# Identity built on GpSimd, the norm's weights loaded as one row and spread by two matmuls of ones

## The chip, the cores and the metric

The kernel runs on one core of one Trainium2 chip. The time is the device time of one execution in microseconds (us); the change is judged by the median of several executions. TensorE is called PE in the profile, VectorE DVE, ScalarE ACT, GpSimd POOL, and SP is the engine that issues most DMAs.

## What is computed

One decoder block on 1024 tokens of width 1024: a SwiGLU half-step, a merge of dilated attention and pooling, a second half-step, and a final norm. Only the first lines matter here, since the change lies in the norm ahead of the first half-step:

```
def rms_norm(x, g):
    xf = x.astype(jnp.float32)
    y = xf * lax.rsqrt(jnp.mean(xf * xf, axis=-1, keepdims=True) + RMS_EPS)
    return (y * g.astype(jnp.float32)).astype(x.dtype)

h = h + 0.5 * swiglu(rms_norm(h, ffn1_norm[l]), ffn1_w1[l], ffn1_w3[l], ffn1_w2[l])
```

`ffn1_norm` holds one weight per channel, 1024 in all. Everything behind this norm is left as it is.

## The kernel before

Tokens are tiled by 128: `h[0]` to `h[7]` hold the rows of `x`, one token per partition, 1024 channels along the partition. The matrix products are done in fp32 split in a high and a low part, by a scheme that multiplies halves (tokens 0 to 511 and 512 to 1023; channels 0 to 511, `LOWS`, and 512 to 1023, `HIGHS`). The first products need the transpose of the LOWS half of the first four row tiles; it is called `b11`.

The order of every engine's instructions in this stage is written out by hand in `begin_up1`. For each row tile t of the first four:

1. `squares(t)`: ACT squares the row and sums it (L274), once the row's DMA has landed.
2. `inverse(t)`: DVE forms mean plus epsilon (L278), POOL raises it to the power -0.5 (L279). The result is the tile `nst`.
3. `rows(t, "b11", LOWS)`: DVE multiplies the half row by `nst` and by the norm's weights (L285, a SCALAR_TENSOR_TENSOR). PE transposes the four 128x128 blocks by a product with the identity `ident` (L407) into a PSUM bank `x_b`. ACT copies the bank into the high part `xhi_b` (L408), and later DVE subtracts to get the low part `xlo_b` (L411, `lower`).

When all four are transposed, `entry.product` starts the first real products (`u_f10a`, L331). Between these steps stand calls of `keep_on(n)`: n products of ones with ones into a bank named `idle` (L916) that nobody reads. Each shows as two MATMUL rows in the profile. PE takes its instructions in order, so what stands behind them waits for them.

The weights have to lie along the free dimension on all 128 partitions for step 3. They come as a 128x8 tile `gain1` (one DMA on ACT's queue, 32 bytes per partition). DVE widens each column to 128 equal columns (`widen`, L920), PE transposes the eight blocks (`gains`, L926), which leaves the weights spread over all partitions in two PSUM banks, one for LOWS and one for HIGHS. DVE copies the first bank into the SBUF tile `gain_row` (L942), ACT later the second (L960). The identity is loaded by a second DMA on ACT's queue (L871).

SP issues the loads of rows and of the first weights, in program order. A DMA takes one of eight semaphores in turn, and is issued when the DMA eight places ahead of it has landed.

SBUF has a left and a right stack of pools. `consts` is the lowest pool on the left. It holds `ident`, `ones`, `mhalf`, `gain1` and two unused tiles named `pad`; the operands `xhi`, `xlo` and the left operands of the down products lie above it.

Of the kernel before, what the change touches and what calls it, by code (L numbers as in the profile page):

```python
# [10 lines left out]
F32 = mybir.dt.float32  # L11
F32R = mybir.dt.float32r
AF = mybir.ActivationFunctionType
OP = mybir.AluOpType
AX = mybir.AxisListType

P = 128
# [3 lines left out]
KT = D // P  # L21
# [116 lines left out]
def tile_block(  # L138
# [28 lines left out]
    nc = tc.nc  # L167
    ve, ac, gp, pe = nc.vector, nc.scalar, nc.gpsimd, nc.tensor

    def sbuf(name, side="left", bufs=1):  # L170
        return tc.tile_pool(name=name, bufs=bufs, side=side, reuse_waits="tile")

    consts = ctx.enter_context(sbuf("consts"))
# [5 lines left out]
    def bank(tag, name):  # L179
        return psum.tile([P, HALF], F32, tag=tag, name=name)  # L180

    def tmp(name):
        return keep.tile([P, 1024], F32, tag="tmp", bufs=TMP_BUFS, name=name)
# [9 lines left out]
    ident = consts.tile([P, P], F32, name="ident")  # L193
    ones = consts.tile([P, P], F32, name="ones")
# [4 lines left out]
    h = []  # L199
# [70 lines left out]
    inv = {}  # L270

    def squares(t, out):
        inv[t] = small.tile([P, 2], F32, tag="nst", name=f"nst_{t}")
        ac.activation(out, h[t], AF.Square, accum_out=inv[t][:, 0:1])  # L274

    def inverse(t):
        st = inv[t]
        ve.tensor_scalar(st[:, 0:1], st[:, 0:1], 1.0 / D, EPS, op0=OP.mult, op1=OP.add)  # L278
        gp.tensor_tensor(st[:, 1:2], st[:, 0:1], mhalf, op=OP.pow)  # L279

    def scaled(t, out, gain):
        ve.scalar_tensor_tensor(out, h[t], inv.pop(t)[:, 1:2], gain, op0=OP.mult, op1=OP.mult)

    def scaled_part(t, c, gain):
        ve.scalar_tensor_tensor(h[t][:, c], h[t][:, c], inv[t][:, 1:2], gain[:, c], op0=OP.mult, op1=OP.mult)  # L285
# [12 lines left out]
    LOWS, HIGHS = slice(0, HALF), slice(HALF, S)  # L298
# [564 lines left out]
                    tick(i)  # L863


    gain1 = consts.tile([P, KT], F32, name="gain1")
    warm = consts.tile([P, 1], F32, name="warm")
    cnt = consts.tile([P, 4, 16], F32, name="cnt")
    psc = consts.tile([P, 4], F32, name="psc")
    nc.scalar.dma_start(gain1, ffn1_norm)  # L870
    nc.scalar.dma_start(ident, c_ident)  # L871
    ac.activation(warm, mhalf, AF.Silu)

    scope = ExitStack()
# [9 lines left out]
    gain_row = keep.tile([P, D], F32, tag="gain", bufs=1, name="gain_ffn1")  # L884
    square = row("square")
    columns_tile = tmp("columns")
    columns = columns_tile.rearrange("p (k c) -> p k c", k=KT)

    def load_all():
        load_rows(0, 1, 2, 3)  # L890
        raws.depth = 2
        raws.load()
        load_rows(4)
        raws.depth = 3
        raws.load()
        load_rows(5)
        raws.depth = 4
        raws.load()
        load_rows(6, 7)
        raws.depth = 6  # L900
        raws.load()

    def pre_run(sv, todo, first, low):
        return Entry(sv, [(*((q.A, m, q.a_out), (q.B, m, q.b_out))[k],) for q, m in todo for k in range(2)], low,
                     lambda n, part=0: first.A.summed(6, part > 1, gp) if part else first.A.operand((6, 7)[n]))

    def begin_up1():


        load_all()  # L910
        idle = bank("mm", "idle")

        def keep_on(n):

            for _ in range(n):
                pe.matmul(idle[:, :P], ones, ones, start=True, stop=True)  # L916

        def widen(b):
            k = slice(4 * b, 4 * b + 4)
            ve.tensor_copy(columns[:, k], gain1[:, k, None].to_broadcast([P, 4, P]))  # L920

        def gains(b):

            p = bank("acc", f"gain{b}")
            for k in range(4):
                pe.transpose(p[:, k * P:(k + 1) * P], columns[:, 4 * b + k], ident)  # L926
            return p

        r = {}

        def rows(t, what, c, tag="acc"):
            scaled_part(t, c, gain_row)
            r[t] = Rows(X, what, h[t][:, c], t, tag)

        keep_on(12)
        widen(0)
        squares(0, square)
        widen(1)
        inverse(0)
        g = [gains(b) for b in range(2)]  # L940
        keep_on(2)
        ve.tensor_copy(gain_row[:, LOWS], g[0])  # L942
        for t in range(1, 4):
            squares(t, square)
        inverse(1)
        rows(0, "b11", LOWS)
        keep_on(2)
        rows(1, "b11", LOWS)
        inverse(2)
        inverse(3)  # L950
        keep_on(2)
        pairs = [Pair(sv1, j, sums, True, j == 2) for j in range(3)]
        entry = pre_run(sv1, [(q, m) for m in (1, 2) for q in pairs[:2]] + [(pairs[2], m) for m in (1, 2)],
                        pairs[0], h[:4])
        entry.operand(0)
        rows(2, "b11", LOWS)
        keep_on(3)
        rows(3, "b11", LOWS, "mm")
        keep_on(2)
        ac.activation(gain_row[:, HIGHS], g[1], AF.Copy)  # L960
        for t in range(4):
            r[t].lower()
        sv1.terms = (0, 2, 1)
        entry.product(0)
        sv1.terms = (0, 1, 2)
        entry.operand(1)
        for t in range(4):
            r[t].keep(h[t][:, LOWS])

        square2 = columns_tile  # L970
        squares(4, square2)
        for t in (0, 1):
            rows(t, "b21", HIGHS)
        entry.product(1)
        entry.out(0)
        entry.operand(2)
        entry.operand(3)
        inverse(4)
        r[0].lower()
        for t in (2, 3):  # L980
            rows(t, "b21", HIGHS)
        for t in (1, 2):
            r[t].lower()
        entry.product(2)
        entry.out(1)
        squares(5, square2)
        r[3].lower()
        for t in range(4):
            r[t].keep(h[t][:, HIGHS])
        entry.product(3)  # L990
        entry.operand(4)
        entry.out(2)
        entry.operand(5)
        entry.out(3)

        def high(t, part):
            if part == 0:
                inverse(t)
                return
            scaled(t, h[t], gain_row)  # L1000
            return h[t]

        def after(t):
            if t + 2 < NT:
                squares(t + 2, square2)
            if t < 6:
                raws.depth = t + 3
                raws.load()

        entry.run(high, after, 4)  # L1010
        return pairs
# [406 lines left out]
    with tc.manual_schedule():  # L1418
# [4 lines left out]
        for k in range(len(items) + 4):  # L1423
# [7 lines left out]
            if k < len(items):  # L1431
                q, m = items[k]
# [3 lines left out]
            if k - 1 in results:  # L1436
                q, m = items[k - 1]
# [358 lines left out]
    def branches():  # L1796
        for n in range(2 * KT):
            yield from branch(n)

    fill = branches()  # L1800
# [65 lines left out]
    first = first_w_o()  # L1866
# [193 lines left out]
    with tc.manual_schedule():  # L2060
# [28 lines left out]
        for i in range(2, STEPS - 4):  # L2089
            step_o(i)  # L2090
            m, st = i // 2 - 1, i % 2
# [13 lines left out]
        m = len(DOWN) - 1  # L2105
# [18 lines left out]
        r = [rows_first2(t) for t in range(2)]  # L2124
# [223 lines left out]
```

## Time and profile before

| | |
|---|---|
| median of 3 runs | 1892.95 us (1892.79 to 1893.48) |
| time of the profiled execution | 1892.07 us |
| its span | 1890.2 us |
| PE busy | 1879.9 us, 99% of the span |
| granted PE clock, mean | 0.999 |
| bytes moved by DMA | 330.79 MB, mean 175 GB/s |

The span is the time from the first to the last record on the core. A row of the timeline has the start in us, the busy time in us, the engine, the line, the operation with out and in, the count of instructions merged into the row, and in brackets the idle time ahead of it with what ended it. A merged row's time runs from its first start to its last end.

### The profile page before, as it was taken

What the parts mean: (1) busy time and instruction counts of PE and PEld (TensorE: products, weight loads), DVE (VectorE), ACT (ScalarE), POOL (GpSimd) and SP (SyncE); (2) the same over time, 40 slices, a digit from 0 to 9 for tenths busy, and PEclk for the clock granted to TensorE, in tenths of its full rate; (3) what the DMA queues carried; (4) which work ended last, traced back from release to release, by engine and by line L of the source; (5) the groups of instructions that cost most, each with busy time, mean ns of one, the idle gap of its engine ahead of it and who ended that gap; (6) DMA issues with size and microseconds to landing.
All of it is one profiled execution on the core that took longest, in us unless ns stands there. A gap on an engine that the chain in (4) does not pass through costs nothing.

```text
span 1890.2 us, 24694 instructions
## 1 busy us (share of the span) xinstructions
PE 1879.9 (99%) x8822; PEld 1561.9 (83%) x8822; DVE 1331.9 (70%) x1975; ACT 772.8 (41%) x1394; POOL 712.2 (38%) x533
## 2 busy tenths in 40 slices
PE   9999999999999999999999999999999999999998
PEld 8888888888888888888888888888888888888887
DVE  6776556657786777557885896887665566577867
ACT  7323333333334553334445772363333323334344
POOL 5433333331223254444555357543333333312221
PEclk9999999999999999999999999999999999999999
DMA  5154223436566526765668968744332223454654
GB/s 191 60 198 166 84 89 106 139 111 216 170 224 210 183 84 210 236 219 188 224 236 314 322 224 289 270 153 149 140 127 103 84 102 118 137 189 162 226 197 145
DMA packets 144019, 330.79 MB, mean 175 GB/s; under 512 B 17560, under 2 KB 39064, under 8 KB 142360
## 3 DMA queue, kind: packets, MB, share of 16 engines
q1 hardware_dynamic: 140152, 318.36, 48.6%
q10 hardware_dynamic: 3744, 10.85, 1.6%
q8 instruction: 70, 1.15, 0.3%
q14 instruction: 53, 0.43, 0.1%
HBM read 229.61 MB, written 99.55 MB: 174 GB/s over the span
## 4 chain that ended last, share of the span: by engine, by line
PE 57%; DVE 2%; ACT 1%; DMA 1%; issue 0%; POOL 0%; ACTq 0%; DVEq 0%; SPq 0%
PE u_mixm L331 15%; PE d_f L815 11%; PE wo L2028 4%; PE yp L1770 1%; PE u_f20b L331 1%; PE u_f21a L331 1%; PE u_f210b L331 1%; PE u_f210a L331 1%; PE u_f29b L331 1%; PE u_f29a L331 1%; PE u_f28a L331 1%; PE u_f27b L331 1%; PE u_f27a L331 1%; PE u_f26b L331 1%; PE u_f26a L331 1%; PE u_f25b L331 1%
## 5 line engine op out<-in xcount | busy, mean ns | idle before, releaser
L815 PE MATMUL d_f<-bhi_f,ahi_f 128*128 128x512 f32 x616 | 240.2, 390 | 0.0
L815 PE MATMUL d_f<-bhi_f,alo_f 128*128 128x512 f32 x616 | 239.7, 389 | 0.0
L815 PE MATMUL d_f<-blo_f,ahi_f 128*128 128x512 f32 x616 | 239.6, 389 | 0.0
L772 POOL TENSOR_TENSOR alo_f<-g_f,ahi_f 128x512 fp32r<-128x512 f32 x60 | 85.9, 1448 | 270.0 <-ACT ahi_f L768 270.0
L331 PE MATMUL u_mixm<-xhi_t_mix,wc_mixm 128*128 128x512 f32 x608 | 157.3, 391 | 0.1
L815 PEld LDWEIGHTS d_f<-bhi_f,ahi_f 128*128 128x128 f32 x616 | 115.7, 188 | 24.2 <-ACT h L415 0.5
L815 PEld LDWEIGHTS d_f<-bhi_f,alo_f 128*128 128x128 f32 x616 | 115.6, 188 | 24.2
L815 PEld LDWEIGHTS d_f<-blo_f,ahi_f 128*128 128x128 f32 x616 | 115.7, 188 | 23.7
L331 PEld LDWEIGHTS u_mixm<-xhi_t_mix,wc_mixm 128*128 128x128 f32 x608 | 113.5, 188 | 23.9 <-ACT wc_mixm L319 0.7
L331 PE MATMUL u_mixm<-xhi_b_mix,wc_mixm 128*128 128x512 f32 x456 | 120.4, 391 | 0.0
L322 POOL TENSOR_TENSOR wc_mixm<-s_mixm,wc_mixm 128x512 fp32r<-128x512 f32 x52 | 76.6, 1475 | 104.9 <-ACT wc_mixm L319 94.0
L331 PEld LDWEIGHTS u_mixm<-xhi_b_mix,wc_mixm 128*128 128x128 f32 x456 | 84.9, 188 | 17.3
L319 ACT ACTIVATE wc_mixm<-s_mixm 128x512 fp32r<-128x512 f32 x76 | 47.0, 628 | 109.4 <-DVE s_mixm L373 54.6
L768 ACT ACTIVATE ahi_f<-g_f 128x1024 fp32r<-128x1024 f32 x84 | 81.9, 975 | 3.1 <-DMA g_f<-gs_f 2.0
L331 PE MATMUL u_mixm<-xlo_t_mix,wc_mixm 128*128 128x512 f32 x304 | 81.3, 389 | 0.0
L322 POOL TENSOR_TENSOR wc_mixm<-raw,wc_mixm 128x512 fp32r<-128x512 f32 x40 | 60.2, 1505 | 40.8 <-ACT wc_mixm L319 32.4
L2028 PE MATMUL wo<-w_o,o_hi 128*128 128x512 f32 x224 | 69.3, 390 | 0.0
L768 ACT ACTIVATE bhi_f<-s_f2w 128x512 fp32r<-128x512 f32 x55 | 33.0, 628 | 86.3 <-DVE s_f2w L790 67.6
L768 ACT ACTIVATE bhi_f<-s_f1w 128x512 fp32r<-128x512 f32 x55 | 33.1, 629 | 83.4 <-DVE s_f1w L790 70.2
L331 PEld LDWEIGHTS u_mixm<-xlo_t_mix,wc_mixm 128*128 128x128 f32 x304 | 57.1, 188 | 12.0
L772 DVE TENSOR_TENSOR alo_f<-g_f,ahi_f 128x1024 fp32r<-128x1024 f32 (+1 forms) x48 | 57.6, 1200 | 7.6 <-ACT ahi_f L768 7.5
L331 PE MATMUL u_mixm<-xlo_b_mix,wc_mixm 128*128 128x512 f32 x228 | 61.0, 389 | 0.0
(1332 smaller groups left out, 4751.9 us busy)
## 6 DMA issues: line engine op xcount, KB each, us to landing
g_f<-gs_f SPq DMA_DIRECT2D x70, 512.0 KB
gs_f<-y_f SPq DMA_DIRECT2D x88, 256.0 KB
raw<-in_w2a_dram SPq DMA_DIRECT2D x35, 512.0 KB
raw<-in_w2b_dram SPq DMA_DIRECT2D x35, 512.0 KB
gs_f<-gb_f SPq DMA_DIRECT2D x46, 256.0 KB
raw<-in_w1a_dram SPq DMA_DIRECT2D x22, 512.0 KB
raw<-in_w3a_dram SPq DMA_DIRECT2D x22, 512.0 KB
raw<-in_w1b_dram SPq DMA_DIRECT2D x22, 512.0 KB
```

The lines of the kernel that those rows point to most:

```text
L319: ac.activation(w[:, 0], src, AF.Copy)
L322: eng.tensor_tensor(w[:, 1], src, w[:, 0].bitcast(F32), op=OP.subtract)
L331: pe.matmul(p, a, b, start=(start and n == 0), stop=(n == 11), skip_group_check=not start)
L768: ac.activation(hi[:, c], src, AF.Copy)
L772: eng.tensor_tensor(lo[:, d], src[:, o], hi[:, d].bitcast(F32), op=OP.subtract)
L815: pe.matmul(self.banks[m][t], l, r, start=(first and q == 0), stop=(last and q == 2))
L1770: pe.matmul(p, a, b, start=(j == 0), stop=(j == 11))
L2028: pe.matmul(banks[m][t], l, r, start=(st == 0 and j == 0 and q == 0), stop=(st == 1 and j == 1 and q == 2))
```

## The change

The identity is made on POOL from the tile of ones (AFFINE_SELECT: keep where partition equals column). The 1024 weights are loaded as one row of 4 KB on one partition (`columns`, in the order p*8+k in which they lie in memory). Two products with a row of ones (contraction over that one partition) spread the row over all partitions into the two PSUM banks; the 512 columns of each are read at a step of 8 elements, 32 bytes, which puts them into channel order. The four scalings of the LOWS half read their weights from the PSUM bank; `gain_row` is filled by ACT afterwards, both halves, for later use. The counts of `keep_on` go from 12 to 7 and from 2 to 3, the banks of x_b 2 come from another tag, and the second scaling stands one `inverse` later. `gain1` is gone, so every tile of the left stack that lies above it starts 32 bytes lower; the right stack is where it was.

```diff
-    gain1 = consts.tile([P, KT], F32, name="gain1")
-    nc.scalar.dma_start(gain1, ffn1_norm)
-    nc.scalar.dma_start(ident, c_ident)
+    gp.affine_select(out=ident, in_=ones, compare_op=OP.is_equal, fill=0.0, base=0, pattern=[[-1, P]],
+                     channel_multiplier=1)
...
-    columns = columns_tile.rearrange("p (k c) -> p k c", k=KT)
+    columns = columns_tile[0:1, :]
+    nc.scalar.dma_start(columns, ffn1_norm.rearrange("(o p) k -> o (p k)", o=1))
...
-        def widen(b):
-            k = slice(4 * b, 4 * b + 4)
-            ve.tensor_copy(columns[:, k], gain1[:, k, None].to_broadcast([P, 4, P]))
-
         def gains(b):
             p = bank("acc", f"gain{b}")
-            for k in range(4):
-                pe.transpose(p[:, k * P:(k + 1) * P], columns[:, 4 * b + k], ident)
+            r = columns.rearrange("o (p k) -> o k p", k=KT)[:, 4 * b:4 * b + 4]
+            pe.matmul(p.rearrange("m (k p) -> m k p", k=4), ones[0:1, :], r, start=True, stop=True)
             return p
...
-        def rows(t, what, c, tag="acc"):
-            scaled_part(t, c, gain_row)
+        def rows(t, what, c, tag="acc", first=None):
+            if first is None:
+                scaled_part(t, c, gain_row)
+            else:
+                ve.scalar_tensor_tensor(h[t][:, c], h[t][:, c], inv[t][:, 1:2], first, op0=OP.mult, op1=OP.mult)
             r[t] = Rows(X, what, h[t][:, c], t, tag)
-        keep_on(12)
-        widen(0)
+        keep_on(7)
         squares(0, square)
-        widen(1)
         inverse(0)
         g = [gains(b) for b in range(2)]
-        keep_on(2)
-        ve.tensor_copy(gain_row[:, LOWS], g[0])
+        keep_on(3)
...
-        rows(0, "b11", LOWS)
+        rows(0, "b11", LOWS, "acc", g[0])
         keep_on(2)
-        rows(1, "b11", LOWS)
         inverse(2)
+        rows(1, "b11", LOWS, "acc", g[0])
         inverse(3)
...
-        rows(2, "b11", LOWS)
+        rows(2, "b11", LOWS, "mm", g[0])
         keep_on(3)
-        rows(3, "b11", LOWS, "mm")
+        rows(3, "b11", LOWS, "mm", g[0])
         keep_on(2)
-        ac.activation(gain_row[:, HIGHS], g[1], AF.Copy)
+        for c, p in zip((HIGHS, LOWS), (g[1], g[0])):
+            ac.activation(gain_row[:, c], p, AF.Copy)
```

On DVE, from the first widening to the fourth scaling, the program before has these rows (x_133 to x_136 are row tiles 0 to 3, and nst_225 to nst_247 their scales):

```order
L920 COPY columns<-gain_109 128x512 x2
L278 TENSOR_SCALAR nst_225<-nst_225 128x1
L942 COPY gain_ffn_141<-gain_230 128x512
L278 TENSOR_SCALAR nst_243<-nst_243 128x1
L285 SCALAR_TENSOR_TENSOR x_133<-x_133,nst_225,gain_ffn_141 128x512
L285 SCALAR_TENSOR_TENSOR x_134<-x_134,nst_243,gain_ffn_141 128x512
L278 TENSOR_SCALAR nst_245<-nst_245 128x1
L278 TENSOR_SCALAR nst_247<-nst_247 128x1
L285 SCALAR_TENSOR_TENSOR x_135<-x_135,nst_245,gain_ffn_141 128x512
L285 SCALAR_TENSOR_TENSOR x_136<-x_136,nst_247,gain_ffn_141 128x512
```

The same place on DVE in the changed program (x_131 to x_134 are row tiles 0 to 3, gain_222 is the PSUM bank of the LOWS weights):

```order
L278 TENSOR_SCALAR nst_218<-nst_218 128x1
L278 TENSOR_SCALAR nst_229<-nst_229 128x1
L931 SCALAR_TENSOR_TENSOR x_131<-x_131,nst_218,gain_222 128x512
L278 TENSOR_SCALAR nst_231<-nst_231 128x1
L931 SCALAR_TENSOR_TENSOR x_132<-x_132,nst_229,gain_222 128x512
L278 TENSOR_SCALAR nst_233<-nst_233 128x1
L931 SCALAR_TENSOR_TENSOR x_133<-x_133,nst_231,gain_222 128x512
L931 SCALAR_TENSOR_TENSOR x_134<-x_134,nst_233,gain_222 128x512
```

The two widenings and the copy of the weights are gone, the scaling of row tile 1 has moved behind the mean of row tile 2, and the last three rows stand in the order they had.

On PE, from the start to the first real product, the program before has these rows:

```order
L916 MATMUL idle<-ones 128x128 x12
L926 MATMUL gain_230<-ident,columns 128x128 x4
L926 MATMUL gain_235<-ident,columns 128x128 x4
L916 MATMUL idle<-ones 128x128 x2
L407 MATMUL x_b_0_252<-ident,x_133 128x128 x4
L916 MATMUL idle<-ones 128x128 x2
L407 MATMUL x_b_1_261<-ident,x_134 128x128 x4
L916 MATMUL idle<-ones 128x128 x2
L407 MATMUL x_b_2_277<-ident,x_135 128x128 x4
L916 MATMUL idle<-ones 128x128 x3
L407 MATMUL x_b_3_287<-ident,x_136 128x128 x4
L916 MATMUL idle<-ones 128x128 x2
```

And in the changed program, at the same place on PE (gain_222 and gain_224 are the two banks of weights):

```order
L916 MATMUL idle<-ones 128x128 x7
L922 MATMUL gain_222<-columns,ones 128x512
L922 MATMUL gain_224<-columns,ones 128x512
L916 MATMUL idle<-ones 128x128 x3
L407 MATMUL x_b_0_238<-ident,x_131 128x128 x4
L916 MATMUL idle<-ones 128x128 x2
L407 MATMUL x_b_1_249<-ident,x_132 128x128 x4
L916 MATMUL idle<-ones 128x128 x2
L407 MATMUL x_b_2_263<-ident,x_133 128x128 x4
L916 MATMUL idle<-ones 128x128 x3
L407 MATMUL x_b_3_273<-ident,x_134 128x128 x4
L916 MATMUL idle<-ones 128x128 x2
```

Only the head of the list differs; from the transposes of row tile 0 on the rows are the same. Behind the first real product the order of all engines is the one before, but for ACT's second copy into `gain_row`, which stands directly behind the first.

## Prediction

> **What bounds the kernel now.** I read the page first: shares of the engines, then the waits of PE.
>
> ```profile
> span 1890.2 us, 24694 instructions
> PE 1879.9 (99%) x8822; PEld 1561.9 (83%) x8822; DVE 1331.9 (70%) x1975; ACT 772.8 (41%) x1394; POOL 712.2 (38%) x533
> PE idle L916 <- DVE mhalf L198: 1.1, 1, 1.1
> PE x_b L407 <- DVE x L285: 0.8, 1, 0.8
> ```
>
> PE is busy for all but 10.3 us of the span, and the two longest of its waits lie in the first 9 us. So the kernel is a row of products that starts late once: a gain or loss is a shift of the first real product, handed on to the end, provided PE finds no new wait behind it. Behind it the change reaches a later stage only by addresses (a rival below). The idle products count as busy, so the page's 99% hides the part that this change works on. I therefore read the timeline up to that product, backwards.
>
> ```profile
> 12.88 2.14 PE L331 MATMUL u_f10a<-xhi_b_f,wc_f10a 128*128 128x512 f32 x8 [0.24 <-ACT xhi_b_f L408]
> 12.23 0.60 ACT L408 ACTIVATE xhi_b_f<-x_b 128x512 fp32r<-128x512 f32 x1 [0.58 <-PE x_b L407]
> 11.54 0.66 PE L407 MATMUL x_b<-ident,x 128*128 128x128 f32 x4
> 10.85 0.83 PE L916 MATMUL idle<-ones 128*128 128x128 f32 x6
> 10.39 0.63 PE L407 MATMUL x_b<-ident,x 128*128 128x128 f32 x4 [0.24 <-issue]
> 10.73 0.75 DVE L285 SCALAR_TENSOR_TENSOR x<-x,nst,gain_ffn 128x512 f32<-128x512 f32 x1 [0.44 <-POOL nst L279]
> 9.69 1.00 POOL L279 TENSOR_TENSOR nst<-nst,mhalf 128x1 f32<-128x1 f32 x1 [0.23 <-DVE nst L278]
> 9.54 0.75 DVE L285 SCALAR_TENSOR_TENSOR x<-x,nst,gain_ffn 128x512 f32<-128x512 f32 x1
> 9.46 0.15 DVE L278 TENSOR_SCALAR nst<-nst 128x1 f32<-128x1 f32 x1 [0.62 <-ACT square L274]
> 9.24 0.19 ACT L274 ACTIVATION_READ_ACCUMULATOR square<-x 128x1 f32 x1
> 8.27 1.06 ACT L274 ACTIVATE square<-x 128x1024 f32<-128x1024 f32 x1
> 7.00 1.06 ACT L274 ACTIVATE square<-x 128x1024 f32<-128x1024 f32 x1 [0.19 <-DMA x<-in_x_dram]
> 5.65 1.06 ACT L274 ACTIVATE square<-x 128x1024 f32<-128x1024 f32 x1 [0.37 <-DMA x<-in_x_dram]
> ```
>
> The product waits for the copy of x_b 3, that for the transposes, those for the scaling of row tile 3, that for POOL's power, that for the sum of squares, which ends at 9.43 behind a string of squares held up twice by the landing of x. The weights and the identity are not on this chain. Their own chain is seen in these rows:
>
> ```profile
> 4.31 0.76 DVE L920 COPY columns<-gain 128x512 f32<-128x512 f32 x2 [3.31 <-DMA gain<-in_ffn_norm_dram]
> 5.88 1.06 PE L926 MATMUL gain<-ident,columns 128*128 128x128 f32 x8
> 6.55 0.69 DVE L942 COPY gain_ffn<-gain 128x512 f32<-128x512 f32 x1 [1.09 <-PE gain L926]
> 7.36 1.41 DVE L285 SCALAR_TENSOR_TENSOR x<-x,nst,gain_ffn 128x512 f32<-128x512 f32 x2
> 8.91 0.55 POOL L279 TENSOR_TENSOR nst<-nst,mhalf 128x1 f32<-128x1 f32 x1 [0.98 <-DVE nst L278]
> ```
>
> They set when row tile 0 is scaled (7.36), but DVE has done tiles 0 and 1 by 8.77 and then waits 0.62 for ACT's third sum (9.46). The gain of this chain is given back there. What the change can move is the landing of x.
>
> **Term 1: the two loads that go.** `gain1` and the identity run on ACT's queue, q10, beside x on q1.
>
> ```profile
> q1 hardware_dynamic: 336, 1.25, 84.6%
> q10 hardware_dynamic: 288, 0.07, 7.6%
> ```
>
> These are the queues from 1.5 to 5.5 us. Of 4 us, 7.6% of all sixteen engines is 0.304 us, in a stretch where x is waited for. The new row brings back 4 KB of these 68 KB, at their price per byte 0.02 us. So x 1 and x 2 land about 0.28 us sooner, if the saving goes to the rows ahead of it; at least nothing, if packets of q10 ran in gaps. ACT then squares row tile 1 at 5.37 and tile 2 at 6.72 instead of 7.00. ACT would be free by 5.37 + 1.27 = 6.64 (8.27 and 7.00 are two starts without a wait between), so the landing still decides. The sum of tile 3 ends at 9.43 - 0.28 = 9.15.
>
> **Term 2: from that sum to the last transposes.** The mean follows at 9.18, the scaling of tile 2 (0.75) starts at 9.26, and its transposes at 10.39 - 0.28 = 10.11. Behind them stand four transposes (10.39 to 10.85: 0.46) and six idle halves. In the row below four halves take 0.61, and the first of the next group starts 0.44 after a group of four started, so six take 0.67.
>
> ```profile
> 6.78 0.61 PE L916 MATMUL idle<-ones 128*128 128x128 f32 x4
> 8.66 0.61 PE L916 MATMUL idle<-ones 128*128 128x128 f32 x4
> 9.10 0.60 PE L407 MATMUL x_b<-ident,x 128*128 128x128 f32 x4
> ```
>
> PE can begin on tile 3 at 10.11 + 0.46 + 0.67 = 11.24. The data is there earlier. POOL's power for tile 3 took 1.00 where it ran beside a scaling that reads both inputs from SBUF, and 0.55 at 8.91 beside none. In the changed kernel that scaling takes its second input from PSUM. So the power ends between 9.41 + 0.55 = 9.96 and 10.41, and the scaling between 10.76 and 11.18; both are ahead of 11.24. The 0.45 us that POOL may win is hidden behind the idle products, and the start moves by 11.54 - 11.24 = 0.30. The Trainium skill (SBUF — State Buffer, Who interferes with whom) says that DVE holds up GpSimd with two SBUF inputs but not with one; by that rule the power takes 0.55, and the sum stays at 0.30. A scaling with its second input in PSUM isn't in the trace; the nearest rows are the 0.75 above and a subtraction with one input in PSUM (0.68), and I take 0.72.
>
> **Term 3: the spread of the row, cost 0.** Seven idle products are 14 halves:
>
> ```profile
> 1.05 4.93 PE L916 MATMUL idle<-ones 128*128 128x128 f32 x24 [1.05 <-DVE mhalf L198]
> ```
>
> 24 took 4.93 us, so 14 end at 1.05 + 14 x 0.205 = 3.92. Each spreading product has 512 columns, four times an idle one, in two halves; the four halves of both cost between 16 x 0.11 = 1.8 (the later pace) and 16 x 0.205 = 3.3 us (the first pace), if the step of 32 bytes costs nothing. They end between 5.7 and 7.2, the idle three behind them (0.67) by 7.9. The row is there by then: 128 packets of `gain1` had landed by 4.31. Tile 0 can be scaled when DVE has formed the mean of tile 1 (its squares now end at 5.37 + 1.06 + 0.19 = 6.6), so from 6.8 to 7.5. Its transposes start by 7.9 instead of 8.16. From tile 0 to tile 2 PE needs 8.16 to 9.98 (9.10, and 0.88 for one more group of each kind), 1.82, then 1.13 to tile 3: 7.9 + 2.95 = 10.85, ahead of 11.24. Nothing waits.
>
> **Term 4: the identity on POOL, cost 0.** POOL has done nothing when the first power starts:
>
> ```profile
> 5.54 0.56 POOL L279 TENSOR_TENSOR nst<-nst,mhalf 128x1 f32<-128x1 f32 x1 [5.10 <-DVE nst L278]
> 13.91 1.78 POOL L322 TENSOR_TENSOR wc_f10b<-raw,wc_f10b 128x512 fp32r<-128x512 f32 x1 [1.30 <-ACT wc_f10b L319]
> ```
>
> No AFFINE_SELECT is in the trace. By the nearest rows it costs between 0.56 (one column, two inputs) and 1.78 (512 columns, held up); it has 128, so I take 0.75. It starts at about 1 us and has 4.5 us to spare; no reason excludes a slower one, and above that it delays the powers (second rival).
>
> **Term 5: ACT's second copy, and who comes first to the shared port.** The copy costs ACT 0.48 (the next two rows start that far apart). Behind it on ACT stand the split of `wc_f10b` and four copies.
>
> ```profile
> 12.72 0.59 ACT L960 ACTIVATE gain_ffn<-gain 128x512 f32<-128x512 f32 x1
> 13.20 0.63 ACT L319 ACTIVATE wc_f10b<-raw 128x512 fp32r<-128x512 f32 x1
> 14.45 1.78 DVE L285 SCALAR_TENSOR_TENSOR x<-x,nst,gain_ffn 128x512 f32<-128x512 f32 x1
> 16.35 0.42 PEld L407 LDWEIGHTS x_b<-ident,x 128*128 128x128 f32 x4 [0.21 <-issue]
> 17.94 1.40 DVE L285 SCALAR_TENSOR_TENSOR x<-x,nst,gain_ffn 128x512 f32<-128x512 f32 x2
> 19.60 1.03 PE L407 MATMUL x_b<-ident,x 128*128 128x128 f32 x8
> ```
>
> Before, POOL comes at 13.91 for the low part of `wc_f10b`. DVE's second scaling of the HIGHS half comes at 14.45 behind it, takes 1.78 instead of 0.75, ends at 16.23, and PE waits 0.21. Now DVE's chain comes sooner: the copy of x_b 3 ends at 12.53, the last subtraction (0.68) at 13.25, and the two HIGHS scalings start at 13.2 and 13.9. ACT's split ends at 13.20 - 0.30 + 0.48 + 0.63 = 14.01, so POOL comes at 14.05, now behind the second scaling. By this order the wait of 0.21 goes. The margin is 0.15 us. Later ACT runs 0.48 - 0.30 = 0.18 late, so the two scalings that start at 17.94 end at 19.52 instead of 19.34, while PE wants the second's result at 19.60 - 0.51 + 0.44 = 19.53; with some 0.1 from end to start, 0.06 to 0.1 is lost again. Term 5 is a gain of about 0.12, between -0.15 (order as before, ACT late) and +0.21.
>
> **Sum.** 0.30 + 0.12 = 0.42 us: the profiled execution goes from 1892.07 to 1891.65. It lies 0.88 under the median of the runs shown; I carry the difference to the median, 1892.95 to **1892.5**. Its bounds: a gain of at most 0.30 + 0.45 (if POOL's gain in term 2 came through as well) + 0.21 = 0.96, at worst 0 - 0.15 = 0.15 slower. A change of under 0.2% (3.8 us) is about what a measurement of this kernel can't tell from no change, so this case is "same" from end to end.
>
> **Rivals.** First, and on the other side: the strided row. PE reads 512 weights at steps of 32 bytes. Tile 3 is late once tile 0 starts after 11.54 - 2.95 = 8.59, so once the four halves end after 7.92, four us behind 3.92: 1.0 us per half against 0.44 at the later pace. From there each further 0.25 us per half costs 1 us of the whole; at four times 0.44 they end at 10.96, tile 3 starts at 14.6, 3.0 us later: 1896.0. Above 1.95 us per half it is over 3.8 us. For it speaks that nothing in the trace reads so from SBUF into PE. Against it speaks the one row that shows the same step, ACT's read of a bank, which for two of three head groups goes by 4 or 8 floats and for the others by one, with no difference:
>
> ```profile
> L1088 ACT ACTIVATE y_m<-u_mixm x19: 577/598/600, 657.6 to 1016.7; 128x512 f32<-128x512 f32 x19
> ```
>
> The Trainium skill (SBUF — State Buffer, Door 1) gives SBUF lines of 16 bytes, at least two hits per line for full rate, and a penalty without a figure for each new line; here every weight is on a new line, so the rule speaks against this change. Chance 0.16, a third of it above 3.8 us.
>
> Second: the identity comes late. If POOL can't finish it before 7.5, the first power ends at 8.06, tile 0 is scaled by 8.85, its transposes start at 8.9, and tile 3's at 11.85, 0.3 us later than now: 1893.25 to 1893.3. The first power started 0.08 us behind its input (5.46), so POOL was ready by then. The Trainium skill (GPSIMD Engine Reference, Instruction dispatch) gives about 6 us for the first call of a freshly loaded library; the row at 5.54 shows less, and by that rule the identity would be late as above. Chance 0.05.
>
> Third: addresses. All operands on the left stack start 32 bytes lower. If that changes the pace of PE's reads, it does so everywhere: 8822 rows times 0.43 ns are 3.8 us, times 1 ns 8.8 us, either way (1884 or 1902).
>
> ```profile
> 1331.35 19.04 PE u_f22a L331 x84
> 1674.06 209.45 PE d_f L815 x924
> ```
>
> In the chain of work both kinds of product take 0.2267 us each, though one has one operand from the left stack and the other two; that speaks against an effect of place, but no row has another offset. Chance 0.16: 0.06 slower by over 3.8 us, 0.06 faster, 0.04 between.
>
> Last: no gain, since q10's packets ran in gaps and the port order stays: 1892.95 to 1893.1, chance 0.05.
>
> **How the numbers follow.** Forecast 0.58, strided row 0.16, addresses 0.16, late identity 0.05, no gain 0.05. Slower by over 0.2%: 0.05 + 0.06 = 0.11; faster 0.06; the rest, 0.83, within. The range starts at the sum's best end, 1892.0, less 0.8 for the spread of the runs shown (0.69) and small effects of addresses: 1891.2. It goes up to 1895.0, where the strided row has lost 2 us. Left out are the far parts of two rivals, about 0.2.
>
> **What would show it.** Right: x 1 and x 2 squared at about 5.37 and 6.72; x_b 3 transposed at 11.24 with the idle products directly ahead of it; `u_f10a` at 12.6; the last power near 0.55 us; no HIGHS scaling over 1 us; the transposes behind `u_f10b` about 0.4 us early. Wrong: L922 rows of over 1 us each, x_b 0 waiting for POOL, or a pace of `u_f22a` other than 0.2267.

## The result and the profile after

The changed kernel takes **1915.88 us** (median of four runs, 1915.82 to 1916.08), the kernel before 1893.22 beside it (1892.79 to 1893.66). The ratio is 1.012, 95% interval 1.0102 to 1.0137: 22.7 us slower, where 1892.5 was forecast and the range ended at 1895.0.

The page of the changed kernel says little by itself, since TensorE is as full as before:

```profile
span 1913.9 us, 24669 instructions
PE 1904.2 (99%) x8810; PEld 1562.2 (82%) x8810; DVE 1333.2 (70%) x1972; ACT 775.0 (40%) x1395; POOL 708.9 (37%) x534
```

Twelve rows of PE fewer take 24.3 us more. Either all is late, or the products run slower; stretches of 50 us tell which. This is the table of windows, one row of the kernel before and then two of the changed one; the number behind x in the second column counts PE's rows.

```profile
400.00:450.00 50.00, 50.00 (x222) 41.42 (x221) 34.32 (x49) 16.60 (x26) 11.06 (x8) 1.00 0.56 191
```

```profile
400.00:450.00 50.00, 50.00 (x216) 40.27 (x215) 28.41 (x40) 17.56 (x28) 15.62 (x11) 1.00 0.44 153
1400.00:1450.00 50.00, 50.00 (x222) 41.43 (x221) 28.98 (x40) 16.66 (x28) 16.48 (x12) 1.00 0.33 118
```

In the first FFN (400 to 450) PE starts 216 products instead of 222 at full granted clock (1.00); in the second FFN the number is the old one. The chain of work that ended last gives the pace of each stage (start, length, what, how many):

```profile
237.75 19.60 PE u_f15b L331 x84
810.58 47.59 PE u_mixm L331 x204
1354.56 19.04 PE u_f22a L331 x84
1697.28 143.55 PE d_f L815 x634
```

The same view of the kernel before has this row for the mixer:

```profile
794.37 46.30 PE u_mixm L331 x204
```

`u_f1` is the first FFN's up-products, `u_mixm` the mixer's; `u_f2` and `d_f` are the second FFN's up-products and the down-products. 19.60 / 84 is 233.3 ns for `u_f1`, and 47.59 / 204 is 233.3 for `u_mixm`, where it was 46.30 / 204 = 227.0. `u_f2` (19.04 / 84 = 226.7) and `d_f` (226.4) are as before. The two slow groups have 22 x 84 + 1596 = 3444 products. Added up over the two traces, from each product's start to the next one's, `u_f1` takes 431.9 us instead of 420.0 and `u_mixm` 373.8 instead of 364.2: together 21.4 us, or 6.2 ns a product.

A smaller part is lost at the start. These are PE's rows in the timeline of the changed kernel, then four rows of other engines:

```profile
4.39 3.99 PE L922 MATMUL gain<-columns,ones 1*128 1x512 f32 x4
8.30 1.65 PE L916 MATMUL idle<-ones 128*128 128x128 f32 x6
9.74 1.06 PE L407 MATMUL x_b<-ident,x 128*128 128x128 f32 x4
10.60 0.99 PE L916 MATMUL idle<-ones 128*128 128x128 f32 x4
11.43 0.60 PE L407 MATMUL x_b<-ident,x 128*128 128x128 f32 x4
13.42 0.60 PE L407 MATMUL x_b<-ident,x 128*128 128x128 f32 x4
14.70 2.13 PE L331 MATMUL u_f10a<-xhi_b_f,wc_f10a 128*128 128x512 f32 x8 [0.24 <-ACT xhi_b_f L408]
18.39 0.94 PE L331 MATMUL u_f10b<-xhi_b_f,wc_f10b 128*128 128x512 f32 x3
```

```profile
1.12 0.29 POOL L869 TENSOR_SCALAR_AFFINE_SELECT ident<-ones 128x128 f32<-128x128 f32 x1 [0.63 <-DVE mhalf L198]
7.24 1.06 ACT L274 ACTIVATE square<-x 128x1024 f32<-128x1024 f32 x1 [0.53 <-DMA x<-in_x_dram]
9.96 0.55 POOL L279 TENSOR_TENSOR nst<-nst,mhalf 128x1 f32<-128x1 f32 x1 [0.75 <-DVE nst L278]
15.29 1.41 DVE L285 SCALAR_TENSOR_TENSOR x<-x,nst,gain_ffn 128x512 f32<-128x512 f32 x2
```

`u_f10a` starts at 14.70 instead of 12.88. The four halves of the spread fill 4.39 to 8.30, 0.98 us each. Then six idle halves take 1.65 where before they took 0.83, and four transposes 1.06 instead of 0.60: half pace, until the next group at 11.43 is at 0.60 again. The idle halves ahead of the spread stand 213 ns apart, as the first ones before did; there they came to 110 ns at about 5.3 us, and here the spread began first. Fourteen halves (6 + 4 + 4) lie between 8.30 and 11.43; at 0.11 us each they would have taken 1.55, so half pace costs 1.6 us of the 1.82. The two parts, 21.4 and 1.8, leave about 0.5 of the 23.75 us between the two profiled executions (1915.82 and 1892.07). The granted clock, third from the end in the table of windows, stands at half there:

```profile
8.00:10.00 2.00, 2.00 (x9) 1.70 (x9) 1.11 (x4) 1.54 (x4) 0.59 (x2) 0.50 1.03 420
```

(The column isn't always so: it reads 1.00 from 1 to 4 us in this trace, and in e2 below through 8 to 12 us, while idle halves stand 213 ns apart. The pace is the better witness.)

### The profile page after: what moved, and what is told of

Same layout as the page of the kernel before. It is cut to its first block, busy times and chain, and to the rows that moved or that the text cites. A ratio compares the mean times of both kernels' runs of the same rounds, so it can differ in the third digit from the quotient of the medians.

```text
span 1913.9 us, 24669 instructions
## 1 busy us (share of the span) xinstructions
PE 1904.2 (99%) x8810; PEld 1562.2 (82%) x8810; DVE 1333.2 (70%) x1972; ACT 775.0 (40%) x1395; POOL 708.9 (37%) x534
## 4 chain that ended last, share of the span: by engine, by line
PE 93%; DVE 3%; ACT 2%; issue 1%; DMA 1%; POOL 1%; ACTq 0%; SPq 0%; DVEq 0%; POOLq 0%
PE u_mixm L331 19%; PE d_f L815 18%; PE wo L2025 4%; PE yp L1767 1%; PE u_f10a L331 1%; PE u_f11a L331 1%; PE u_f12a L331 1%; PE u_f110b L331 1%; PE u_f110a L331 1%; PE u_f19b L331 1%; PE u_f19a L331 1%; PE u_f18b L331 1%; PE u_f18a L331 1%; PE u_f17b L331 1%; PE u_f17a L331 1%
## 5 line engine op out<-in xcount | busy, mean ns | idle before, releaser
L815 PEld LDWEIGHTS d_f<-bhi_f,ahi_f 128*128 128x128 f32 x616 | 115.6, 188 | 24.3 <-ACT h L415 0.4
```

Source lines behind the costliest of these rows:

```text
L815: pe.matmul(self.banks[m][t], l, r, start=(first and q == 0), stop=(last and q == 2))
```

## The experiments

Two theories were put to the test. **Addresses:** dropping the 32 bytes of `gain1` moves everything on the left stack down, and that slows two groups of products. **Start:** the spread from one row makes TensorE late. The rival of the first is that the new start itself makes all later products take longer.

**e1, the old addresses with the new start.**

```
     ident and the identity on GpSimd as after the change
+    consts.tile([P, KT], F32, name="gap")
     warm = consts.tile([P, 1], F32, name="warm")
```

> The kernel after with a tile of 32 bytes, never used, put where the norm's weights stood: every tile of the left stack is back at its old address, and the prologue is the changed one. Theory, addresses: a product whose moving operand starts at 0 and whose stationary operand at 32 bytes past a multiple of 64 is issued every 233.3 ns instead of 226.7, and 3444 products of the first FFN and the mixer stand so after the change. Then both groups go back to 226.7 ns, 222 of PE's rows stand in 50 us between 100 and 450 us instead of 216, and the time is 1893.2 + 1.8 (the later first product) = 1895.0 us, between 1894.3 and 1895.5. Rival, the one-row products or the identity from GpSimd leave TensorE in a slower state: the pace stays at 233.3 ns and the time at 1915.9 us.

Measured 1895.24 us (ratio 1.0012, 1.0003 to 1.0021). The chain of e1:

```profile
232.59 19.04 PE u_f15b L331 x84
796.44 46.30 PE u_mixm L331 x204
```

Both groups are back at 226.7 and 227.0 ns, and `u_f10a` starts at 15.19. The kernel before took 1892.55 beside this run, so 2.7 us of the loss are left: thirty-two unused bytes win back 20.0 of the 22.7 us. The rival of the first theory is dead.

**e3, the old start with the new addresses.**

```
-    consts.tile([P, 32], F32, name="pad2")
+    consts.tile([P, 24], F32, name="pad2")
```

> The kernel before with one change: an unused tile in the constants is 24 floats instead of 32, so the left stack lies 32 bytes lower, as after the change, and the prologue is the old one. Theory, addresses: u_f1 and u_mixm go to 233.3 ns, the others stay at 226.7, the first product stays at 12.88, and the time is 1893.2 + 3444 x 6.6 ns = 1893.2 + 22.7 = 1915.9, at least 1914. Rival, a slower state left by the new prologue: 1893.2.

Measured 1914.00 us against 1892.55 (1.0112, 1.0099 to 1.0126): +21.45, nothing else of the change being there (`u_f10a` starts at 13.03, against 12.88). In the chain of e3:

```profile
235.93 19.60 PE u_f15b L331 x84
1352.46 19.04 PE u_f22a L331 x84
```

So the loss is shown from both sides. It is under the 22.7 us that the forecast had from 3444 x 6.6 ns, because the two groups' mean pace before was 226.9 and 227.2 ns and not 226.7 throughout: added up as above, they take 21.4 us more in e3's trace, as after the change. Alone the two parts cost 21.45 and 2.7 us, together 22.7; the difference of 1.5 is about what the start varies from run to run (e1's runs lie between 1893.77 and 1896.07).

**e2, the row read without its step**, on e1:

```
-            r = columns.rearrange("o (p k) -> o k p", k=KT)[:, 4 * b:4 * b + 4]
+            r = columns.rearrange("o (k p) -> o k p", k=KT)[:, 4 * b:4 * b + 4]
```

> The kernel with the old addresses and the new prologue, its two spreading products reading the row of weights without a step (one weight after the other instead of every eighth); left out is the right order of the norm's weights over the channels. Theory, the step: each of the four halves takes 0.44 to 0.85 us instead of 1.0 to 1.2, the granted clock stays at 1.00 through 8 to 12 us, the first product of u_f10a starts at 12.6 to 13.0 us, and the time is 1892.8 to 1893.6 us. Rival, a product from one row is slow whatever its step, or the clock falls for another reason: halves of 1.0 us, first product at 14.7 and 1895.0 us, as with the step.

Measured 1895.16 us, 1.0012 (1.0003 to 1.0021): no different from e1, so the theory of the step fell. The tile view of e2 (shortest, median and longest; first and last start) and two rows of its timeline:

```profile
L923 PE MATMUL gain<-columns,ones x4: 1056/1056/1217, 4.4 to 7.1; 1*128 1x512 f32 x4
8.09 1.65 PE L917 MATMUL idle<-ones 128*128 128x128 f32 x6
15.43 2.11 PE L331 MATMUL u_f10a<-xhi_b_f,wc_f10a 128*128 128x512 f32 x8 [0.24 <-ACT xhi_b_f L408]
```

The halves still stand 0.85 us apart, and half pace lasts even longer. The rival (the clock) had it.

**e4, 36 pairs of starts, and the read of a row by itself.** A kernel of its own:

```
for s in (0, 16, 32, 48, 64, 96):
    for m in (0, 16, 32, 48, 64, 96):
        ...  # 96 products: st[:, s/4 + 128 (n % 4):][:, :128], mv[:, m/4 + 32 (n % 8):][:, :512]
for parts in (1, P):
    for step in (1, 2, 4, 8):
        r = row[0:parts, :HALF * step].rearrange("p (c k) -> p k c", k=step)[:, 0]
        ...  # 12 products: ones[0:parts, :], r
```

> A kernel of its own that leaves all of the block's work out: 96 products of fp32r 128x512 for each of 36 pairs of starts (stationary and moving operand each at 0, 16, 32, 48, 64, 96 bytes past a multiple of 128), then fp32 products of 512 columns that read one row or 128 rows of SBUF at a step of 1, 2, 4 and 8 floats. Theory, addresses: 226.7 ns each where both starts agree modulo 64 (0 with 64, 32 with 96 too), 233.3 ns where they differ by 32, unknown at 16 and 48. Rival one: only the moving operand's place counts (a whole column of the grid slow). Rival two: the pace needs the traffic of the other engines and DMAs, so all 36 are alike here. For the step: the theory has 128 rows as slow as one row at step 8 and step 1 at 0.4 to 0.5 us a half; the rival (few rows are slow) has one row slow at every step.

As a test of addresses this run failed by its own design: the moving operand went on by 128 bytes from product to product, and nearly every group mixed paces, mostly between 224 and 241 ns, with means of 228 to 233. The theory's 226.7 where both starts agree modulo 64 did not come (231 with both at 0), and no column was slow as a whole, which rival one wanted. The groups differ though no other engine worked, so rival two is out. The mixture showed that what counts is not the two starts modulo 64, and led to e5. The reads at a step are plain. Timeline of e4, 24 halves a row, tiles named by step and rows:

```profile
811.14 17.70 PE L209 MATMUL r1k1x<-row,ones 1*128 1x512 f32 x24
870.72 22.25 PE L209 MATMUL r8k1x<-row,ones 1*128 1x512 f32 x24
892.90 12.23 PE L209 MATMUL r1k128x<-row,ones 128*128 128x512 f32 x24
904.97 10.96 PE L209 MATMUL r2k128x<-row,ones 128*128 128x512 f32 x24
915.77 21.76 PE L209 MATMUL r4k128x<-row,ones 128*128 128x512 f32 x24
937.35 22.21 PE L209 MATMUL r8k128x<-row,ones 128*128 128x512 f32 x24
```

From 128 rows a half takes 0.45 us at a step of 2 floats, and 0.90 and 0.92 at 4 and 8 (start to start). The Trainium skill (SBUF — State Buffer, Door 1) names lines of 16 bytes that want two hits each and gives the penalty no figure; here two floats to a line cost next to nothing and one to a line doubles the time. At a step of 8 a half takes 0.92 from one row at a granted clock of 0.50 and 0.92 from 128 rows at 1.00 alike: with the step, the clock no longer matters to the spread itself. So the theory of the step and its rival both held: the step costs at 1 and at 128 rows, and one row came to be slow at every step. From one row without a step, the first seven halves stood 0.43 to 0.53 us apart and the later ones 0.85, though TensorE never paused. The window of that time:

```profile
820.00:830.00 10.00, 10.00 (x13) 3.98 (x12) 0.00 (x0) 0.00 (x0) 0.00 (x0) 0.50 0.00 0
```

After some 3.5 us of one-row products the clock is halved, and after some 3.5 us of 128-row products it is whole again (the first four halves of r1k128x stand 0.76 to 1.02 apart, the others 0.43). The Trainium skill (TensorE: Matmul & The Clock Gate, The HAM clock gate) says that half clock is the default, and that one busy window of about 3.4 us lifts it. The trace agrees on the time, and adds what the page does not say: a product from one row doesn't count as busy.

**e5, one distance at a time.** As e4, but both operands step by multiples of 512 bytes, so that the distance between moving and stationary start stays the same modulo 512 within a group.

> A kernel of its own that leaves the block's work out, as e4, but now the distance of the moving from the stationary operand stays the same within a group: both step by multiples of 512 bytes, as the kernel's own operands do, and the distance goes through 0, 16, 32 ... 496 bytes modulo 512 (96 products each), some of them again with both operands 32 bytes higher. The kernel's own traces show 226.7 ns at a distance of 0 and of 256, and 233.3 ns at 480 (that is -32). Theory, a distance: those three come again, with either start, and other distances have other paces, between 225 and 237. Rival, only the start modulo 64: every multiple of 64 gives 226.7. A distance below 226 ns would be a way to a faster kernel.

Timeline of e5; d is the distance, b how far both are moved:

```profile
56.15 22.57 PE L205 MATMUL d32b0x<-mv,st 128*128 128x512 f32 x96
100.95 22.15 PE L205 MATMUL d64b0x<-mv,st 128*128 128x512 f32 x96
279.07 22.56 PE L205 MATMUL d192b0x<-mv,st 128*128 128x512 f32 x96
324.00 22.56 PE L205 MATMUL d224b0x<-mv,st 128*128 128x512 f32 x96
346.40 21.93 PE L205 MATMUL d240b0x<-mv,st 128*128 128x512 f32 x96
368.17 21.96 PE L205 MATMUL d256b0x<-mv,st 128*128 128x512 f32 x96
812.69 22.55 PE L205 MATMUL d224b32x<-mv,st 128*128 128x512 f32 x96
```

From the start of one group to the next, 96 products at 224 take 346.40 - 324.00 = 22.40 us (233.3 ns each) and at 240 368.17 - 346.40 = 21.77 (226.8). Inside the groups the mean pace is 226.7 to 227.1 at 240, 256 and 496, and at 0 with both operands 32 bytes higher (227.9 in the very first group, which has one product of 319 ns); 229.0 at 64 and 320; 233.3 to 233.4 at 32, 192, 224 and 480; 234.7 at most. The row repeats after 256 bytes, and moving both operands by 32 bytes changes nothing. So it is the **distance modulo 256 bytes**. Of the distances tried none is faster than 226.7, so none is a way to a faster kernel.

**e6, 64 bytes lower instead of 32**, in the kernel before:

```
-    consts.tile([P, 32], F32, name="pad2")
+    consts.tile([P, 16], F32, name="pad2")
```

> The kernel before with the unused tile of 32 floats cut to 16: the left stack lies 64 bytes lower, so starts modulo 64 are all as before, but the distance of the moving from the stationary operand in u_f1 and u_mixm becomes -64. Theory, a distance modulo 256: both groups get a pace other than 226.7, by the groups of e4 with steps of 128 bytes some 230 ns, so 1893 + 3444 x 3.3 ns = 1904 us, between 1898 and 1917. Rival, the start modulo 64: 1892.5 to 1893.3, as before.

Measured 1914.91 us against 1892.87 (1.0117, 1.0104 to 1.0131). The pace was 233.3 ns, as e5 has it at 192, not the 230 taken from e4's mixtures (chain of e6):

```profile
237.16 19.60 PE u_f15b L331 x84
```

All starts were what they had been modulo 64, so that rival is dead. (In its trace the two groups take 21.6 us more, and the start 1.1: x 2 landed late, and `u_f10a` starts at 14.01.) By the addresses that the program gives its tiles, the distance in the kernel before is a multiple of 256 for `u_f1`, `u_mixm`, `u_f2`, `d_f` and `wo` (the attention's output products) alike: the first product of `u_f10a` reads X at byte 36064 of the partition and weights at 118752, and 82688 is 323 x 256. After the change X is at 36032 and the weights are where they were. Of these groups the change makes the distance -32 for the two whose X lies on the left stack and whose weights lie on the right one; `u_f2` and `d_f` have both operands on the left, `wo` both on the right. One smaller group, the 192 products of `yp`, moves to -32 as well; it takes 0.2 us longer in all.

**e11, the edges, and what else could matter**: as e5, in steps of 4 bytes, then with the same stationary columns each time, then with fewer moving columns.

> As e5, the block's work left out: products at distances of 224 to 272 bytes in steps of 4; then at 0 and 32 with the same stationary columns loaded each time; then at 0 and 32 with 128 and 256 moving columns instead of 512. Theory, the two reads meet in a part of the memory that repeats every 256 bytes: there is a window of distances about 240 to 256 in which the pace is 226.7, with its edges between 224 and 240 and between 256 and 272; the same columns each time change nothing (226.7 and 233.3, or one of the paces of e5); a short product loses as much per product as a long one, about 6.6 ns. Rival, single lucky distances: only 240 and 256 are fast.

The theory of a window fell, the rival was nearer. Timeline of e11:

```profile
79.19 21.93 PE L203 MATMUL d236x<-mv,st 128*128 128x512 f32 x96
122.71 23.20 PE L203 MATMUL d244x<-mv,st 128*128 128x512 f32 x96
167.84 21.93 PE L203 MATMUL d252x<-mv,st 128*128 128x512 f32 x96
```

At 236, 240, 252 and 256 the pace is 226.7 to 226.8, between them it is 239.9 (244) and 230.1 (248), and 236.6 at 260. The same columns each time gave 226.9 and 233.4, as expected. Products of 128 columns lost nothing at a distance of 32 (111.1 both), and of 256 columns were faster (118.4 against 120.4). So the forecast of one loss per product fell. But 128 and 256 columns take nearly the same time, so something other than the columns paces these short products, and a loss could be hidden behind it: it is shown for 512 columns alone.

**e7, e9 and e10: clock and step taken apart**, each on e1. In e7 the row lies in a tile of zeros and the products read 128 rows; in e9 there are twelve idle products ahead of them, as before the change; e10 is e9 without the step.

```
e7  +    ve.memset(columns_tile, 0.0)
    +    nc.scalar.dma_start(columns[0:1, :], ...)
    +            pe.matmul(p.rearrange(...), ones, r, start=True, stop=True)
e9  -        keep_on(7)
    +        keep_on(12)
e10      e9, with the row read as in e2
```

> e1_gap with the row of weights put into a tile whose other 127 partitions are zero, so that the two spreading products read 128 rows instead of one, at the same step of 32 bytes. Theory, the clock: TensorE runs at half pace (213 ns a half product of 128 columns) until some 4 us of full products are behind it, and products of one row don't count; now they count, so idle and x_b run at 110 ns from about 5.5 us on. The four halves still take 0.92 us each for their step, tile 0 is transposed at 8.9, tile 3 at about 11.9, u_f10a starts at 13.2 instead of 15.2, and the time is 1892.6 + 0.3 = 1892.9 us, at most 1893.5. Rival, the step alone costs the time: 1895.2, as e1_gap.

> e1_gap with twelve idle products of 128 rows ahead of the two spreading products, as the kernel before has, instead of seven. Theory, two causes of which each is enough: TensorE comes to full pace at 5.3 to 6.5 us (24 idle halves end at 6.2), but the four halves still take 0.9 us each for their step of 32 bytes, so they end at about 10 us, two of the idle and x_b groups later run at 110 ns, and u_f10a starts at 14 to 15.3: 1894.5 to 1895.5 us. Rival, the clock alone: halves of 0.43 us, u_f10a at 13 and 1892.9 us.

> e9_warm with the row read without its step, as in e2 (the weights' order over the channels is left wrong). Theory, two causes: now neither is there, the halves take 0.43 us once the clock is up (one or two of them 0.85 if it comes late), end at about 8 us, tile 0 is transposed at 8.5, and u_f10a starts at 12.6 to 13.4, set by when the rows of x land: 1892.4 to 1893.4 us, as the kernel before. Rival, one-row products pull the clock down again at once: halves of 0.85, x_b at 213 ns, u_f10a at 15 and 1895 us.

e7 took 1895.64 us (1.0015, 1.0006 to 1.0024), not 1892.9. Its timeline (ACT's queue first):

```profile
2.16 0.52 ACTq L889 DMA_DIRECT2D columns<-in_ffn_norm_dram  x1
6.37 3.99 PE L924 MATMUL gain<-columns,ones 128*128 128x512 f32 x4 [1.92 <-DMA columns<-in_ffn_norm_dram]
10.19 0.85 PE L918 MATMUL idle<-ones 128*128 128x128 f32 x6
```

The clock did what was expected: idle halves at 0.11 right behind the spread. But the row's load now waits for the zeros, is issued at 2.16 instead of 0.78, and PE waits for it until 6.37. With the step, 0.92 a half, `u_f10a` started at 15.03. Without the wait of 1.92 it would have been 13.11 by estimate, near the 13.2 of the theory; no run shows that. The mechanism is shown, its price isn't isolated.

e9 took 1896.84 us (1.0023, 1.0014 to 1.0032), worse than either forecast. e10 took 1894.04 (1.0008, 0.9999 to 1.0017), between its two. One row of e9, then three of e10:

```profile
10.12 1.65 PE L917 MATMUL idle<-ones 128*128 128x128 f32 x6
```

```profile
5.93 1.98 PE L923 MATMUL gain<-columns,ones 1*128 1x512 f32 x4
8.61 1.02 PE L407 MATMUL x_b<-ident,x 128*128 128x128 f32 x4
14.62 2.12 PE L331 MATMUL u_f10a<-xhi_b_f,wc_f10a 128*128 128x512 f32 x8 [0.24 <-ACT xhi_b_f L408]
```

In e9 the clock was up before the spread (an idle half at 0.12 at 5.96), and four halves at 0.92 brought it down again until 16.24. In e10, with clock and no step, a half takes 0.43 (the prediction's lower price was 0.44); yet the x_b transposes behind are at half pace from 8.78 on, and x 2 landed late (squared at 8.55). So step and clock each keep the spread slow, and even a fast spread from one row costs clock afterwards.

**e8, the change without its row** (the identity on GpSimd and the scalings from PSUM, weights by channel as before), **and e12, the identity alone**:

```
-    nc.scalar.dma_start(ident, c_ident)
+    gp.affine_select(out=ident, in_=ones, compare_op=OP.is_equal, fill=0.0, base=0, pattern=[[-1, P]],
+                     channel_multiplier=1)
e8 also
-        ve.tensor_copy(gain_row[:, LOWS], g[0])
-        rows(0, "b11", LOWS)
+        rows(0, "b11", LOWS, "acc", g[0])
         ...
```

> The kernel before with the identity made on GpSimd and the first scalings reading the weights from PSUM, but the weights still loaded by channel and turned by the eight transposes, at the old addresses: the change without its row. Theory: the row, by step and clock, is all that the prologue lost; without it the prediction's first two terms come: the power of tile 3 takes 0.55 instead of 1.00 us, x_b 3 is transposed at 11.2 instead of 11.5, u_f10a starts at 12.4 to 12.7, and the time is 1892.1 us, between 1891.7 and 1892.6 where the kernel before has 1892.55. Rival, the scalings from PSUM or ACT's second copy cost something themselves: 1893 or more.

> The kernel before with one change: the identity is made on GpSimd and its load is gone; addresses, weights and scalings are as before. The prediction's first term has x 1 and x 2 land 0.3 us earlier for it (squares at about 5.4 and 6.7), which gives 1892.2 us where the kernel before has 1892.5. Theory after eleven runs: in the traces with the load x 2 is squared at 7.00, 7.05 and 8.13, without it at 7.24 to 8.55, so the load was not what x waited for, and SP's later loads, issued sooner, take its place: the square at 7.2 to 8.5, u_f10a at 12.9 to 14, and 1892.5 to 1893.3 us, no gain.

e8 took 1893.06 against 1892.87 and e12 1893.18 against 1892.94, both 1.0001 (0.9992 to 1.0010). The forecast of e8 (1891.7 to 1892.6) fell and that of e12 came: x 2 was squared later than before in both, and `u_f10a` starts at 13.46 and 13.29 instead of 12.88. Neither gains, so no version here beats the kernel before. One row of e8, then two of e12:

```profile
10.36 0.55 POOL L279 TENSOR_TENSOR nst<-nst,mhalf 128x1 f32<-128x1 f32 x1 [0.71 <-DVE nst L278]
```

```profile
7.41 1.06 ACT L274 ACTIVATE square<-x 128x1024 f32<-128x1024 f32 x1 [0.71 <-DMA x<-in_x_dram]
10.10 1.00 POOL L279 TENSOR_TENSOR nst<-nst,mhalf 128x1 f32<-128x1 f32 x1 [0.21 <-DVE nst L278]
```

In both the power of tile 3 starts 0.15 us behind a scaling on DVE. With that scaling's second input in PSUM it takes 0.55 (after the change too), without it 1.00 (before and in e6 too). This fits a port that the two engines share. But the order counts as well: where the power starts only 0.01 to 0.02 us behind a scaling with both inputs in SBUF, it takes 0.55 (at 9.76 in e3, at 7.38 in the kernel before). So the price shows only where the scaling has a head start, which no run varied by itself. It doesn't matter here, because x 2 lands when it lands (squared at 7.69 in e8, 7.41 in e12, 7.00 before).

## Why the prediction was wrong

**The step that failed is the price of the shifted addresses: the sum has no term for it.** The shift was left to the third rival, which had the right 32 bytes and an open sign, and was given 0.06 for a loss of over 3.8 us. The runs put it at 21.4 us (e3's 21.45, and 20.0 won back in e1), against a gain of 0.42 for all of the sum's terms together. It was argued down by one observation: `u_f22a` and `d_f` have the same pace, "though one has one operand from the left stack and the other two". The runs show two faults in that. Both groups have both operands on the left stack, so the pair couldn't differ, and the change leaves both alone. And it asked whether a place is slow, where the distance of two operands decides: in the kernel before every large group stands at a multiple of 256 bytes, so its trace holds no second value. A uniform pace was read as indifference; it was one and the same distance everywhere. The price was mis-sized too: 0.43 to 1 ns a row over all rows, where 6.2 ns on 3444 of them were lost. Consequently the witness named at the end, a pace of `u_f22a` other than 0.2267, was the wrong one: it stayed.

**Term 1 (0.28 us sooner) failed.** q10's share went (0.3% instead of 7.6% from 1.5 to 5.5 us), q1's rose from 84.6% to 92.3%, and x 2 did not come sooner; x 1 was squared 0.09 us earlier, at 5.56. x 2 was squared at 7.00, 7.05 and 8.13 in the three traces with the identity's load (before, e3, e6), and between 7.24 and 8.55 in eight without. SP issued x 4 at 3.60 instead of 4.30 after the change; that its later loads took the free share fits this, but is only argued. What the traces do show is a scatter of a microsecond in one landing, over three times the term that was built on it.

**Term 2** had POOL's power right (0.55 at 9.96) and the scaling nearly (0.75, taken as 0.72). That x_b 3 waits for PE and not for its data was right as well; when PE comes to it was wrong, since PE was late from the spread on: 13.42, not 11.24.

**Term 3 (cost 0) failed** in two ways: a half took 0.98 us, not 0.44 to 0.82, and pace was lost behind it. The two paces that it used (0.205 and 0.11 us an idle half) were taken for the ends of a range. They were the two states of the clock, and the change took away the work that moves TensorE from one to the other: five of the twelve idle products, with products in their place that don't count.

**The strided-row rival** had the place and the right size of a half (its threshold, 1.0 us), and missed the clock. What was held against it, ACT's reads of a bank, was a read of PSUM by another engine; TensorE's own read of SBUF doubles at a step of 16 bytes (e4). By its own rule, halves that end at 8.30 instead of 7.92 cost 0.38; with the 1.6 us at half pace, tile 3 comes at 11.54 + 0.38 + 1.58 = 13.50, and it came at 13.42.

**Term 4** was right and cheaper: 0.29 us at 1.12, and the late-identity rival is dead. The 6 us for a first call that the Trainium skill (GPSIMD Engine Reference, Instruction dispatch) gives are not seen in this instruction.

**Term 5** was right: the two scalings take 1.41 with POOL behind them (0.74 and 1.78 before), and `u_f10b` follows `u_f10a` by 3.69 instead of 3.88. The gain of 0.19 (0.12 forecast) drowns in the rest.

## What to carry to other kernels

Before a tile is dropped or resized, list which operands of the large products move against each other and compare their distances modulo 256 bytes; a dummy of the same size keeps them. A pace that is the same everywhere shows that nothing differs yet, not that nothing matters. Products that read one row neither warm TensorE nor keep it warm, so don't trade warm-up products for them.

## What the runs showed of the hardware

- Products of 128x512 (fp32r) are issued every 226.7 ns at distances of 0, 236, 240 and 252 bytes modulo 256 between moving and stationary operand, and every 228.9 to 239.9 ns at the others tried. The next weights are loaded while a product runs (PEld is busy for 40 of 50 us in the window shown), so the two reads could meet in the memory; that is only argued, and no run took the load away. The Trainium skill (TensorE: Matmul & The Clock Gate, Step-by-step: what each phase is for) says that loading the next tile's weights doesn't steal read bandwidth from the running product. These runs differ by up to 6% with the distance of the two reads; whether the load is the cause they don't show, so they neither confirm the page nor refute it.
- One-row products at full speed (0.43 us a half) halve the granted clock after some 3.5 us without a pause (e4). In e10 less was enough: 1.9 us of them, and half pace set in 0.9 us later, in the middle of products of 128 rows.
- A step of 16 or 32 bytes doubles TensorE's read of 512 fp32 columns from 128 rows (0.90 and 0.92 us a half against 0.43), a step of 8 bytes doesn't (0.45).
